# Output projection of a hybrid Conformer/MLA encoder: weights as two k tiles by 512 columns, products 512 wide, blocks, loads, norms and turns in another order

## The chip, the cores and the metric

The kernel runs on one core of one Trainium2 chip. Time is device time in microseconds (us), from the first to the last instruction of the program and what the launch adds around them. Three runs of the kernel before gave 1146.32, 1147.17 and 1148.84 us; the median is 1147.17 us. The engines are called PE (TensorE), DVE (VectorE), ACT (ScalarE), POOL (GpSimd) and SP (SyncE, which issues the loads and stores).

## The reference

Two sequences of 512 tokens with 16 meta tokens in front go through one encoder layer of width 1024. What matters here is the middle of it:

```python
u = jax.nn.silu(_layernorm(u, conv_ln_g[i], conv_ln_b[i]))        # 512 channels of the convolution
o = _mla_attention(...).reshape(b, l, MLA_HEADS * V_DIM)           # 512 channels of the attention
h = h + jnp.concatenate([u, o], axis=-1) @ w_out[i]                # output projection: 1024 x 1024
hf = _rms(h, ffn_norm_g[i])
h = h + (jax.nn.silu(hf @ w_gate[i]) * (hf @ w_up[i])) @ w_down[i] # feed-forward
```

Everything is float32. The meta tokens' rows are not needed behind the attention, so the output projection has 1024 tokens.

## The kernel before, in words

**Products.** A float32 product is made of three products of float32r parts: each operand is split in a high part (ACT, a cast) and a low part (DVE or POOL, a subtraction), and `mm3` (L151) issues high x high, high x low, low x high for every k tile of 128. All TensorE work of this kind stands under L158 in the profile. Names of a matmul are out<-moving,stationary.

**Output projection.** The stationary operand is 128 tokens by 128 channels of the mixed channels (`act`, or `cq` memory for the first sequence's attention channels), the moving operand is the weight. The weights are eight tiles of 128 x 1024, `wo[2 * dq + half]`: four k tiles by 256 output columns, `dq` being the quarter of the output columns and `half` the half of the channels (0 the convolution's, 1 the attention's). One `w_out_block(half, dq, t)` (L838) makes 128 tokens by 256 columns: 4 k tiles x 3 = 12 matmuls of 256 columns into one of four PSUM banks (`bank`), and DVE adds the result to the residual rows `hres[t]` (L844). There are 8 token tiles; tile t and tile t + 4 are the same rows of the two sequences. Tile 0 of the attention half is made ahead, between the steps of the last attention head (`early_blocks`, L718), in another PSUM tile, and added at L862.

**Weight buffers.** `pair` (L134) loads a tile (SP), casts it (ACT, L141) and subtracts (POOL, L144). Its high and low tiles have four buffers each (tags `pairh`, `pairl`), and a raw tile has two. The four weight tiles of the attention half are loaded during the attention; each of the other four takes a buffer whose user is done, behind each quarter of the attention half (L865). The feed-forward's operands (`Unit.comb`, L948) and the operands of the last stage use the same four and four buffers.

**Order.** First come the 28 blocks of the attention half (quarter by quarter, 7 token tiles), with the steps of the convolution's layer norm, its transposes and silu put between them by a table of positions 0 to 31 (L847-L865). Then come the 32 blocks of the convolution half (L1005-L1031), and between them:

- `ffn_norm(t)` (L876): store of the residual rows (SP), squares (ACT, L182), scale (POOL, L183 and L184), the normed rows in `hf2[t // 4]` (DVE, L881). There is one such tile for each sequence, so the norm of tile t + 1 waits for the turn of tile t.
- `ffn_turn(t)` (L883): 16 transposes on PE (L892) of the normed rows of t and t + 4, and the operands of the feed-forward's block products for these 128 tokens: copies and casts on ACT (L899, L903, L904, L913), sums and low parts on DVE (L900, L905, L908, L909, L911), low parts of four more on POOL (L914).
- `units[0].load()` and `units[0].comb(j)`: the seven weight operands of the feed-forward's first unit. For this unit the low halves are made on DVE (L961), for all later ones on POOL; four temporaries are made on DVE (L946).
- Behind the last norm the first unit's seven products over the tokens of turns 0 and 1 (256 columns), `ffn_turn(3)`, and then the same seven over the tokens of turns 2 and 3. From the second unit on, products are 512 columns wide.

The order written in the program is a priority: a planner that simulates a timeline orders the instructions of each engine, so an instruction whose operands are early can stand ahead of one written before it. [...]

## Time and profile before

| | before |
|---|---|
| median of three runs | 1147.17 us |
| span of the profiled execution | 1145.0 us |
| median less span (what lies around it) | 2.2 us |
| PE busy in the span | 1084.7 us, 95% |
| DVE busy | 828.9 us, 72% |
| POOL busy | 623.9 us, 54% |
| ACT busy | 522.2 us, 46% |
| output projection in the trace | first block at 363.4 us, last product at 463.2 us |
| first product 512 wide of the feed-forward | 497.1 us |

Times inside the profile are from the span's first instruction. A row of a timeline gives start, duration, engine, line, operation, names, shapes, and in brackets the idle time of the engine before it and what ended it. A row of a group gives count, busy time, mean duration in ns and the idle time before. [...]

### The profile page before, as it was taken

Reading aid. Unit: us, or ns where it says so; the run is one execution under the profiler, and the core shown is the slowest. Engines: PE = TensorE matmul, PEld = TensorE weight load, DVE = VectorE, ACT = ScalarE, POOL = GpSimd, SP = SyncE. Lnnn points to the kernel's source line nnn. Section 1 sums busy time; section 2 is a strip of 40 time slices with the busy share of each in tenths; the row PEclk is TensorE's granted clock in tenths of the full one; section 3 lists DMA queues with packets and bytes.
Section 4 is the critical chain, followed back from the end, with each engine's and each line's share of the span. In section 5 each row is a group of like instructions: output and inputs, shape, how many; then the busy total and the mean of one; then the engine's idle time right before and its main releaser. Section 6 shows DMA issues by size and latency. Waiting matters only on the chain. (4 is left out here: it accounts for less than half of the span.)

```text
span 1145.0 us, 15928 instructions
## 1 busy us (share of the span) xinstructions
PE 1084.7 (95%) x5886; PEld 931.5 (81%) x5886; DVE 828.9 (72%) x1142; ACT 522.2 (46%) x928; POOL 623.9 (54%) x499
## 2 busy tenths in 40 slices
PE   4999999999989999899999999999999999998797
PEld 4999887888878999788888888888888777787585
DVE  5699997888886547994555455545553868979998
ACT  6455525786874535643333333333333354343325
POOL 6489725563651323584544454445443586465955
PEclk9999999999999999899999999999999999999998
DMA  7211111010111312323231223122313963110103
GB/s 277 80 38 37 46 47 57 30 56 1 38 38 57 129 37 94 134 81 98 74 110 56 92 74 111 56 93 73 111 47 105 382 246 122 37 37 19 56 1 147
DMA packets 38556, 98.02 MB, mean 86 GB/s; under 512 B 4544, under 2 KB 4800, under 8 KB 38480
## 3 DMA queue, kind: packets, MB, share of 16 engines
q1 hardware_dynamic: 38480, 97.02, 25.0%
q8 instruction: 46, 0.75, 0.3%
q14 instruction: 30, 0.25, 0.1%
HBM read 77.08 MB, written 19.92 MB: 85 GB/s over the span
## 5 line engine op out<-in xcount | busy, mean ns | idle before, releaser
L158 PE MATMUL pt<-act_h,wc 128*128 128x512 f32 (+1 forms) x552 | 176.2, 382 | 0.1
L961 POOL TENSOR_TENSOR wc<-tt,wc 128x512 fp32r<-128x512 f32 x84 | 110.7, 1319 | 101.0 <-ACT wc L959 65.4
L1092 POOL TENSOR_TENSOR wd<-re,wd 128x512 fp32r<-128x512 f32 x69 | 113.4, 1660 | 51.4 <-ACT wd L1090 51.3
L959 ACT CAST wc<-tt 128x512 fp32r<-128x512 f32 x88 | 54.5, 622 | 152.9 <-PE pt L158 150.1
L158 PEld LDWEIGHTS pt<-act_h,wc 128*128 128x128 f32 x552 | 103.3, 190 | 19.9 <-issue 0.3
L158 PE MATMUL pt<-wd,wd 128*128 128x512 f32 x444 | 106.7, 395 | 9.0 <-DVE wd L1092 4.9
L158 PE MATMUL pt<-act_l,wc 128*128 128x512 f32 (+1 forms) x276 | 105.6, 383 | 3.5 <-DVE act_l L900 3.4
L158 PEld LDWEIGHTS pt<-wd,wd 128*128 128x128 f32 x444 | 84.1, 190 | 29.3 <-DVE wd L1092 6.2
L158 PE MATMUL ps<-wd,wd 128*128 128x512 f32 x396 | 96.1, 397 | 10.9 <-DVE wd L1092 7.3
L1090 ACT CAST wd<-re 128x512 fp32r<-128x512 f32 x120 | 68.2, 619 | 81.9 <-PE ps L158 29.9
L158 PEld LDWEIGHTS ps<-wd,wd 128*128 128x128 f32 x396 | 74.8, 191 | 29.7 <-DVE wd L1092 9.3
L144 POOL TENSOR_TENSOR wl<-raw,wh 128x1024 fp32r<-128x1024 f32 x28 | 68.8, 2456 | 51.3 <-ACT wh L141 51.1
L158 PE MATMUL pt<-hn_h,wh 128*128 128x256 f32 (+2 forms) x288 | 92.7, 324 | 1.1 <-ACT hn_h L148 1.1
L158 PE MATMUL pt<-hn_l,wh 128*128 128x256 f32 (+2 forms) x288 | 93.3, 324 | 0.0
L158 PE MATMUL pt<-hn_h,wl 128*128 128x256 f32 (+2 forms) x288 | 92.6, 322 | 0.0
L597 POOL TENSOR_SCALAR p<-p,sst 128x512 f32<-128x512 f32 x64 | 44.0, 693 | 67.2 <-DVE sst L595 59.3
L1092 DVE TENSOR_TENSOR wd<-re,wd 128x512 fp32r<-128x512 f32 x51 | 58.4, 1158 | 21.8 <-ACT wd L1090 21.8
L961 POOL TENSOR_TENSOR wc<-raw,wc 128x512 fp32r<-128x512 f32 x30 | 39.7, 1326 | 43.9 <-ACT wc L959 43.9
L158 PEld LDWEIGHTS pt<-act_l,wc 128*128 128x128 f32 x276 | 52.4, 190 | 13.6 <-DVE act_l L900 3.6
L314 POOL TENSOR_TENSOR pacc<-pacc,prod 128x512 f32<-128x512 f32 x43 | 58.3, 1355 | 7.0 <-ACT prod L312 4.3
L158 PEld LDWEIGHTS pt<-hn_h,wh 128*128 128x128 f32 x288 | 54.6, 191 | 6.0 <-ACT hn_h L148 1.5
L158 PE MATMUL pt<-s4h,wc 128*128 128x512 f32 (+1 forms) x184 | 58.4, 380 | 0.9 <-DVE h L976 0.9
(310 smaller groups left out, 3070.9 us busy)
## 6 DMA issues: line engine op xcount, KB each, us to landing
raw<-in_w_gate_dram SPq DMA_DIRECT2D x22, 512.0 KB, 3.7
g_dram<-slots SPq DMA_DIRECT2D x44, 256.0 KB, 2.4
re<-g_dram SPq DMA_DIRECT2D x40, 256.0 KB, 5.3
re<-in_w_down_dram SPq DMA_DIRECT2D x40, 256.0 KB, 5.4
raw<-in_w_in_dram SPq DMA_DIRECT2D x12, 512.0 KB, 3.9
slots<-in_w_up_dram SPq DMA_DIRECT2D x11, 512.0 KB, 3.5
h<-in_w_up_dram SPq DMA_DIRECT2D x11, 512.0 KB, 3.5
x<-in_x_dram SPq DMA_DIRECT2D x8, 512.0 KB, 5.0
```

The source lines that it names most:

```text
L144: nc.gpsimd.tensor_sub(lo[:, a], raw[:, a], hi[:, a].bitcast(F32))
L158: nc.tensor.matmul(out_ap, lhsT=w_, rhs=m_, start=first and i + j == 0, stop=last and i == n - 1 and j == 2)
L314: nc.gpsimd.tensor_add(acc, acc, to)
L597: nc.gpsimd.tensor_scalar(pr[:, real], pr[:, real], st[:, 2, t:t + 1], 1.0, op0=ALU.mult, op1=ALU.mult)
L959: nc.scalar.copy(w[:, 0:512], src)
L961: lo_eng.tensor_sub(w[:, 512:1024], src, w[:, 0:512].bitcast(F32))
L1090: nc.scalar.copy(w[:, 0:512], a)
L1092: eng.tensor_sub(w[:, 512:], a, w[:, 0:512].bitcast(F32))
```

## The change

The weight tiles become two k tiles by 512 columns, `wo[4 * half + 2 * e + k // 2]`, with `e` the half of the output columns; `w_out_rows` picks the k tile. A block is 128 tokens by 512 columns: again 12 matmuls and one add, each twice as wide, and half as many blocks. The tiles 4 to 7 (attention half) are loaded during the attention, two at a time, as before. Tiles 0 and 1 are loaded when the first column half of the attention blocks is done, tiles 2 and 3 when the second is. The layer norm's table keeps its positions; a block now stands for two. In the second part the blocks, `ffn_norm`, `ffn_turn` and `comb` are written in another order. The computation and its sums over k are the same.

```diff
+    def w_out_rows(half, e, k):
+        return tuple(wx[:, k % 2 * 512:(k % 2 + 1) * 512] for wx in wo[4 * half + 2 * e + k // 2])
...
-            for dq in range(4):
-                if dq == 0:
+            for e in range(2):
+                if e == 0:
                     early.append(bank2())
-                out_ap = early[t][:, dq // 2, dq % 2 * 256:(dq % 2 + 1) * 256]
                 cs = slice(t * 128, (t + 1) * 128)
-                for k0 in (0, 2):
-                    mm3(out_ap, [(o_first[0][:, k, cs], o_first[1][:, k, cs]) for k in (k0, k0 + 1)],
-                        [tuple(wx[:, k * 256:(k + 1) * 256] for wx in wo[2 * dq + 1]) for k in (k0, k0 + 1)],
-                        first=k0 == 0, last=k0 == 2)
+                for k in range(4):
+                    mm3(early[t][:, e, :], [(o_first[0][:, k, cs], o_first[1][:, k, cs])], [w_out_rows(1, e, k)],
+                        first=k == 0, last=k == 3)
                     yield
...
-            for n in (4 * WO_AT.index(h) + 1, 4 * WO_AT.index(h) + 3):
+            for n in (4 + 2 * WO_AT.index(h), 5 + 2 * WO_AT.index(h)):
                 wo[n] = pair(w_out[n])
...
-    def w_out_block(half, dq, t):
-        s, cs, ds = t // 4, slice(t % 4 * 128, t % 4 * 128 + 128), slice(dq * 256, (dq + 1) * 256)
+    def w_out_block(half, e, t):
+        s, cs, ds = t // 4, slice(t % 4 * 128, t % 4 * 128 + 128), slice(e * 512, (e + 1) * 512)
         pt = bank()
-        w = wo[2 * dq + half]
-        mm3(pt[:, :256], [(act[half][s][0][:, k, cs], act[half][s][1][:, k, cs]) for k in range(4)],
-            [tuple(wx[:, k * 256:(k + 1) * 256] for wx in w) for k in range(4)])
-        nc.vector.tensor_add(hres[t][:, ds], pt[:, :256], hres[t][:, ds])
+        mm3(pt, [(act[half][s][0][:, k, cs], act[half][s][1][:, k, cs]) for k in range(4)],
+            [w_out_rows(half, e, k) for k in range(4)])
+        nc.vector.tensor_add(hres[t][:, ds], pt, hres[t][:, ds])
...
-    for dq in range(4):
+    for e in range(2):
         for t in range(8):
             if t >= EARLY:
-                w_out_block(1, dq, t)
-            if dq * 8 + t >= EARLY_AT and early:
+                w_out_block(1, e, t)
+            at = 2 * (e * 8 + t)
+            if at >= EARLY_AT and early:
                 i = EARLY - len(early)
                 nc.vector.tensor_add(hres[i], early.pop(0).rearrange("p a b -> p (a b)"), hres[i])
-            for f, a in steps.pop(dq * 8 + t, ()):
+            for f, a in steps.pop(at, []) + steps.pop(at + 1, []):
                 f(*a)
-        wo[2 * dq] = pair(w_out[2 * dq])
+        for n in (2 * e, 2 * e + 1):
+            wo[n] = pair(w_out[n])
...
-    def w_out_rest(dqs, ts):
-        for dq in dqs:
-            for t in ts:
-                w_out_block(0, dq, t)
-
-    w_out_rest(range(3), (0, 4, 1, 5))
+    for t in (0, 4, 1, 5):
+        w_out_block(0, 0, t)
     for t in (0, 4):
-        w_out_block(0, 3, t)
+        w_out_block(0, 1, t)
         ffn_norm(t)
-    w_out_block(0, 3, 1)
-    w_out_block(0, 3, 5)
+    w_out_block(0, 1, 1)
+    w_out_block(0, 1, 5)
     ffn_turn(0)
     ffn_norm(1)
     ffn_norm(5)
     units[0].load()
-    w_out_rest((0,), (2, 6, 3, 7))
+    for t in (2, 6):
+        w_out_block(0, 0, t)
     ffn_turn(1)
     units[0].comb(0)
     units[0].comb(1)
-    w_out_rest((1,), (2, 6, 3, 7))
+    for t in (2, 6):
+        w_out_block(0, 1, t)
+        ffn_norm(t)
     units[0].comb(2)
     units[0].comb(3)
-    w_out_rest((2,), (2, 6, 3, 7))
-    w_out_block(0, 3, 2)
-    ffn_norm(2)
-    w_out_block(0, 3, 6)
-    ffn_norm(6)
-    w_out_block(0, 3, 3)
+    for t in (3, 7):
+        w_out_block(0, 0, t)
     ffn_turn(2)
-    ffn_norm(3)
-    w_out_block(0, 3, 7)
-    ffn_norm(7)
+    for t in (3, 7):
+        w_out_block(0, 1, t)
+        ffn_norm(t)
     for j in range(4, 7):
         units[0].comb(j)
     for j in range(7):
         units[0].product(j, slice(0, 256))
     ffn_turn(3)
     units[1].load()
...
-    w_out = _pack(a["w_out"][0], KD, 256).reshape(4, 128, 2, 1024).transpose(0, 2, 1, 3).reshape(8, 128, 1024)
+    w_out = np.ascontiguousarray(a["w_out"][0].reshape(2, 2, 2, 128, 2, 512).transpose(0, 4, 1, 3, 2, 5)).reshape(8, 128, 1024)
```

The rest of the diff takes comments and docstrings away.

## The prediction

> **What bounds the kernel now.** I read the page's engine totals first, then a table of stages around the output projection, then who PE waited for there, then the timelines of PE and DVE.

> ```profile
> span 1145.0 us, 15928 instructions
> PE 1084.7 (95%) x5886; PEld 931.5 (81%) x5886; DVE 828.9 (72%) x1142; ACT 522.2 (46%) x928; POOL 623.9 (54%) x499
> core 0: us, PE busy (x) PEld busy (x) DVE busy (x) ACT busy (x) POOL busy (x), PEclk, DMA share, GB/s
> 364.00:411.70 47.70, 46.95 (x394) 46.28 (x393) 26.64 (x61) 26.30 (x40) 12.73 (x17) 1.00 0.34 122
> 411.70:440.60 28.90, 28.90 (x245) 28.90 (x244) 14.06 (x28) 6.31 (x11) 5.15 (x7) 1.00 0.24 92
> 440.60:468.00 27.40, 25.82 (x216) 25.45 (x215) 27.34 (x38) 16.62 (x31) 14.59 (x14) 1.00 0.21 78
> 468.00:497.00 29.00, 22.05 (x162) 20.70 (x160) 27.96 (x34) 18.80 (x35) 17.88 (x16) 0.88 0.27 91
> 497.00:540.00 43.00, 42.93 (x189) 35.59 (x190) 28.45 (x34) 15.28 (x27) 27.22 (x20) 1.00 0.30 98
> ```

> The averages say PE. The stages say more: up to 440.6 us PE has no gap (28.90 of 28.90) and DVE is half idle. From 440.6 to 497.0 it is the other way round: DVE is busy 27.34 + 27.96 = 55.3 of 56.4 us, and PE stands still for 1.6 + 7.0 us, with a granted clock of 0.88. From 497 on PE is gapless again. So two limits follow each other: PE until the first turns, DVE until the second unit's products. Who ended PE's waits there:

> ```profile
> PE pt L158 <- DVE act_l L900: 3.4, 1, 3.4
> PE px L892 <- ACT act_h L899: 1.9, 1, 1.9
> PE pt L158 <- DVE h L844: 1.5, 1, 1.5
> PE pt L158 <- DVE h L976: 0.9, 1, 0.9
> ```

> All but one are DVE, and every one is a late instruction of a full list, not a slow one.

> **The products.** What one block costs is read from the spacing of blocks in a gapless stretch. DVE's adds follow PE block by block, and three blocks of 256 columns lie between these two rows; the PE rows below them are the first matmuls of two neighbouring products of 12 matmuls 512 columns wide.

> ```profile
> 426.27 0.42 DVE L844 TENSOR_TENSOR slots<-pt,slots 128x256 f32<-128x256 f32 x1 [1.02 <-PE pt L158]
> ...
> 430.59 0.42 DVE L844 TENSOR_TENSOR h<-pt,h 128x256 f32<-128x256 f32 x1 [1.02 <-PE pt L158]
> 551.58 0.39 PE L158 MATMUL pt<-s4h,wc 128*128 128x512 f32 x1
> ...
> 554.29 0.39 PE L158 MATMUL pt<-act_h,wc 128*128 128x512 f32 x1
> ```

> A narrow block is 4.32 / 3 = 1.44 us (120 ns a matmul), a wide one 2.71 us (226 ns). Two narrow ones against a wide one: 2.88 - 2.71 = 0.17 us. How many there are:

> ```profile
> L158 PE MATMUL pt<-wh,act_h 128*128 128x256 f32 x192 | 54.5, 285 | 1.6 <-DVE h L844 1.5
> L158 PE MATMUL pt<-wh,cq_h 128*128 128x256 f32 x48 | 13.8, 288 | 0.0
> L158 PE MATMUL ps<-wh,cq_h 128*128 128x256 f32 x16 | 4.6, 288 | 0.0
> ```

> Each row is one of the three parts, so 3 x 256 = 768 matmuls, 64 narrow blocks, become 32 wide ones: 32 x 0.17 = 5.4 us of PE's time, 2.7 us of it ahead of the second part (4 blocks made early and 28 of the attention half), 2.7 us in the second part. The bounds: nothing, if a wide matmul with these operands costs two narrow ones; 5.4 us by the rows. I take the rows, since the shapes are the same and only tile names differ. [...]

> **The adds.** Sixty adds of 256 columns become thirty of 512. Nearest rows for the wide add are the feed-forward's, PSUM plus SBUF, same shape:

> ```profile
> L844 DVE TENSOR_TENSOR slots<-pt,slots x40: 399/423/426, 374.7 to 466.6; 128x256 f32<-128x256 f32 x40
> L844 DVE TENSOR_TENSOR h<-pt,h x20: 409/417/425, 371.0 to 461.2; 128x256 f32<-128x256 f32 x20
> L994 DVE TENSOR_TENSOR slots<-pt,slots x33: 674/680/692, 512.7 to 902.3; 128x512 f32<-128x512 f32 x33
> ```

> 60 x 0.42 = 25.2 us against 30 x 0.68 = 20.4 us. In the crowded stretch, behind turn 0, stand 14 narrow adds (5.9 us) before and 8 wide ones (5.4 us) after: 0.5 us. DVE's list in its full stretch hardly gets shorter.

> **The loads.** Eight of 512 KB as before. The last one before the change was cast and subtracted when the attention half was done:

> ```profile
> 411.97 0.42 DVE L844 TENSOR_TENSOR slots<-pt,slots 128x256 f32<-128x256 f32 x1
> 412.12 1.05 ACT L141 CAST wh<-raw 128x1024 fp32r<-128x1024 f32 x1
> 413.25 2.60 POOL L144 TENSOR_TENSOR wl<-raw,wh 128x1024 fp32r<-128x1024 f32 x1 [7.99 <-ACT wh L141]
> ```

> Now two (tiles 2 and 3) come at that place: 1.05 + 2 x 2.5 = 6.1 us until the second low part. The first block that reads them is the fifth, 4 x 2.71 = 10.8 us on; the four blocks of column half 0 hide it with 4.7 us to spare, and if that cover were gone PE would wait 6.1 us. On SP the first unit's gate loads wait for these two raw tiles, the second of them one more subtraction (2.5 us); nothing on PE reads them before the first `comb`. The norms' stores move with the norms; on SP they stand behind those gate loads, which are out by 409.1 + 6.1 = 415.2 us, while the first norm comes some 14 us (five wide blocks) after 409.1. The two casts at the middle of the attention half put 5 us in a row on POOL ahead of the last layer norms' scales; PE has other blocks to do there, and I allow 0 to 1 us. I take these edits at nothing.

> **The order.** When does DVE's full stretch begin? With the first turn, whose two norms must be there:

> ```profile
> 432.03 0.42 DVE L844 TENSOR_TENSOR slots<-pt,slots 128x256 f32<-128x256 f32 x1 [1.01 <-PE pt L158]
> 435.29 1.29 DVE L881 SCALAR_TENSOR_TENSOR hf<-slots,rs,gain 128x1024 f32<-128x1024 f32 x1 [0.43 <-POOL rs L184]
> 436.99 1.04 PE L892 MATMUL px<-ident,hf 128*128 128x128 f32 x8
> ```

> Before: the residual of tile 4 is complete in its 14th block of the second part; from that add to the end of its norm it is 435.29 + 1.29 - 432.03 = 4.6 us, and the turn starts at 436.99. After: the attention half ends at 411.8 - 2.7 = 409.1 us. Tile 4 is complete with the sixth wide block, 409.1 + 6 x 2.71 = 425.4, its norm 0.3 + 4.6 us later, 430.3. The turn stands behind the eighth block on PE, 409.1 + 21.7 = 430.8, and its operands are just there. So the turn starts at 430.8 instead of 436.99: 6.2 us sooner, of which 3.5 us are the products and the rest the earlier norms.

> Behind it DVE has the same list (turns, norms, the first unit's combinations), 0.5 us shorter. If it stays full, its end moves with its beginning, and so does the second unit's first product:

> ```profile
> 497.07 0.47 PE L158 MATMUL pt<-act_h,wc 128*128 128x512 f32 x1
> ```

> It goes from 497.1 to about 490.9. Behind it the table has PE without a gap, so the shift goes through to the end.

> The sum: -6.2 for the stretch's start, -0.5 for the adds, +0.5 for the loads' bound and the new order's own small waits: -6.2 us. Against the span of 1145.0 us that is 1138.8; around the span lie 1147.17 - 1145.0 = 2.2 us, so **1141.0 us** as a median.

> **Rivals.**

> *PE becomes the bound: the stalls go as well.* PE's own work from the attention half's end is 16 x 2.71 + 8 groups of transposes at 0.8 (436.99 to the next matmul) + 14 products at 1.44 = 70.0 us; 409.1 + 70.0 = 479.1 instead of 497.1, 18 us less. For it: turn 2 now stands two wide blocks ahead of the end instead of one narrow one, so the last turns' chains start earlier. Against it: DVE's 55 us of work must then fit between 431 and 479. A third to two thirds of what lies between (8 to 14 us) gives 1133 to 1139. [...]

> *The first unit's operands come too late, and only the wide products' gain ahead of the turns remains.* Its seven weight operands need the four and four buffers that the projection's weights hold. Before, two came free with each quarter; now tiles 0 and 1 are read until block (0, 0, 7), the 14th of 16, and tiles 2 and 3 until the last. So four combinations written behind turn 1 can only be made some 8 us before the first product, and three only behind the last block.

> ```profile
> 447.16 0.68 DVE L961 TENSOR_TENSOR wc<-raw,wc 128x512 fp32r<-128x512 f32 x1
> ...
> 454.36 2.38 DVE L961 TENSOR_TENSOR wc<-tt,wc 128x512 fp32r<-128x512 f32 x2
> ...
> 462.99 0.28 PE L158 MATMUL pt<-act_h,wc 128*128 128x256 f32 x1
> ```

> Here the first ones were made at 447.16, 16 us before the first product at 462.99. DVE's work is not more by it, but PE would idle at the first products, in place of the waits of 1.9 and 3.4 us behind them. If PE then loses another 3 to 6 us, the gain is 0 to 3 us: 1144 to 1147.

> *Slower: DVE and POOL get in each other's way more often.* DVE's instructions with both operands in SBUF take much longer while POOL works:

> ```profile
> 440.66 0.69 DVE L900 TENSOR_TENSOR act_l<-h,act_h 128x512 fp32r<-128x512 f32 x1 [1.58 <-ACT act_h L899]
> 449.63 1.62 DVE L900 TENSOR_TENSOR act_l<-h,act_h 128x512 fp32r<-128x512 f32 x1
> 449.42 1.29 POOL L914 TENSOR_TENSOR s2l<-h,s2h 128x512 fp32r<-128x512 f32 x1 [3.26 <-ACT s2h L913]
> ```

> The same instruction takes 0.69 us with POOL idle and 1.62 beside L914: 0.9 us more. The change pushes seven L961 and the first unit's operands into the time in which turns 1 and 2 have POOL make low parts. The forecast's 6.2 us are gone with 7 more such meetings, and it is slower by more than noise from 10; 12 of them, of some 40 such instructions, give 1147.2 - 6.2 + 10.8 = 1152.

> *Wide products cost two narrow ones.* The lower bound above: the attention half then ends at 411.8 as before, the eighth block at 411.8 + 23.0 = 434.8, and the turn is 2.2 us sooner by the order alone, 1145.0. Against it stands every product behind 497 us, at 226 ns. [...]

> *The change doesn't do what it says.* The planner may order blocks, norms and turns otherwise than written, and only the products' 5.4 us, or part of them, would show. It lies inside the forecast's range.

> **How the numbers follow.** Forecast (a gain of 3 to 8 us, 1139 to 1144): 0.57. PE bound (more than 8): 0.15. Late operands (0 to 3): 0.16. Wide products at twice the price (1145): 0.03. Slower: 0.09. The range reaches from 1136.0 (half of the PE case) to 1147.0 (all of the late operands). A difference of 0.2%, 2.3 us, is about what a measurement of this kernel can tell. Below 1144.9 lie the forecast, the PE case and a quarter of the late operands: 0.76. Within 0.2%: the rest of the late operands, the twice-price case and a little of the slower case: 0.16. Slower: 0.08.

> **What the profile after would show.** Products: 384 matmuls of 128x512 in the projection, spaced 226 ns; at twice 120 ns the 5.4 us are wrong. Adds: 30 of 128x512 at 0.68. Loads: PE never waits for L141 or L144. Order: the first L892 near 431 us, the full stretch of DVE from about 434 to 491, the first wide feed-forward product near 491. If that product moves far more than the first L892, PE was the bound; if it moves less, the waits say whether it was L961 (late operands) or long L900, L908 and L961 beside POOL. Wrong altogether: a gap of PE in the attention half, or a stage behind 540 us that changes its own length by more than 1 us.

## The result, and the profile after

The changed kernel takes 1155.68 us as a median (1153.76 to 1155.80); the kernel before, timed beside it, 1148.01 us (1146.32 to 1149.06). The ratio is 1.0068, with a 95% interval of 1.0055 to 1.0081: **slower by 7.8 us**, where 1141.0 us and a gain of 6.2 us had been forecast. The profiled execution of the changed kernel took 1153.76 us and spans 1152.0 us; that of the kernel before spans 1145.0 us, so the profiles show 7.0 us of it.

The lines of the program have moved by one to three: the residual's add is L845, the norm's transposes L805 and back L825, its copy back L826, the silu L830 with its parts L832 and L833, the turn's transposes L895, the unit's temporaries L949, its low parts L964, the sums behind the products L979 to L993.

The table of stages of the changed kernel, cut at the attention half's last instruction on PE, the first turn, the first unit's middle and the second unit's first product (columns: stretch, length, busy time of PE, PEld, DVE, ACT and POOL with the count of instructions, granted clock, that is the share of TensorE's full clock, DMA share, GB/s):

```profile
span 1152.0 us, 15137 instructions
364.00:408.40 44.40, 44.40 (x222) 36.77 (x221) 21.19 (x41) 19.43 (x28) 13.33 (x14) 1.00 0.33 115
408.40:439.80 31.40, 24.44 (x100) 19.50 (x98) 13.94 (x22) 9.91 (x16) 3.83 (x9) 0.84 0.21 82
439.80:468.00 28.20, 27.09 (x146) 23.01 (x145) 23.97 (x25) 19.81 (x35) 14.82 (x15) 1.00 0.14 57
468.00:501.70 33.70, 25.60 (x182) 24.39 (x181) 32.55 (x44) 18.74 (x36) 22.01 (x15) 0.89 0.36 118
501.70:545.00 43.30, 43.30 (x186) 35.67 (x186) 26.99 (x31) 14.06 (x25) 25.01 (x19) 0.96 0.28 91
```

The second row is new. Before, PE had no gap from 411.7 us to the first turn and beyond; now it stands still for 7.0 us there, at a clock of 0.84. Whom PE waited for between 400 and 505 us (total, times, longest; the two smallest left out):

```profile
PE pt L158 <- ACT act_h L832: 4.1, 1, 4.1
PE pt L158 <- DVE h L979: 3.3, 1, 3.3
PE ps L825 <- ACT xs L817: 2.8, 2, 2.5
PE pt L158 <- DVE slots L993: 2.2, 1, 2.2
PE pt L158 <- DVE wc L964: 1.1, 1, 1.1
PE pt L158 <- POOL s1l L917: 1.1, 1, 1.1
```

The first and the third row are the convolution's layer norm, which cost PE nothing worth naming before (0.7 us for one of its transposes). The second row stood in the table before with 0.9 us, as `h` of L976. The runs below that take these three waits away, and with them the halved clock behind, win back the loss and more.

Where the 7.0 us of the profiles arise, by three marks:

| | before | after | difference | forecast |
|---|---|---|---|---|
| first turn's first transpose | 436.99 | 439.77 | +2.8 | -6.2 |
| from there to the second unit's first product | 60.1 | 61.7 | +1.6 | 0 (-0.5 + 0.5) |
| from there to the end of the span | 647.9 | 650.5 | +2.6 | 0 |

So the forecast missed by 9.0 us ahead of the first turn, by 1.6 in the crowded stretch, and by 2.6 behind it. The first mark is kind to the changed kernel: the profile before has a stretch at half clock at 340.2 us, ahead of the projection, which the one after lacks. A later profile of the kernel before with one edit behind the first turn (the last run below) has no such stretch, the same list up to there, and its first turn at 435.53 us.

### The profile page after: what moved, and what is told of

It is laid out like the page before. It is cut to its first block, busy times and chain, and to the rows that moved or that the text cites. A ratio compares the mean times of both kernels' runs of the same rounds, so it can differ in the third digit from the quotient of the medians.

```text
span 1152.0 us, 15137 instructions
## 1 busy us (share of the span) xinstructions
PE 1086.5 (94%) x5502; PEld 916.3 (80%) x5502; DVE 823.1 (71%) x1112; ACT 522.2 (45%) x928; POOL 628.6 (55%) x499
## 5 line engine op out<-in xcount | busy, mean ns | idle before, releaser
L158 PE MATMUL pt<-act_h,wc 128*128 128x512 f32 (+1 forms) x552 | 177.8, 385 | 1.7 <-DVE wc L964 1.1
L964 POOL TENSOR_TENSOR wc<-tt,wc 128x512 fp32r<-128x512 f32 x84 | 110.6, 1317 | 103.0 <-ACT wc L962 69.7
L158 PEld LDWEIGHTS pt<-act_h,wc 128*128 128x128 f32 x552 | 104.4, 192 | 22.4 <-DVE wc L964 1.3
L158 PE MATMUL pt<-wd,wd 128*128 128x512 f32 x444 | 108.0, 399 | 8.7 <-DVE wd L1090 4.8
L158 PEld LDWEIGHTS pt<-wd,wd 128*128 128x128 f32 x444 | 85.3, 193 | 29.2 <-DVE wd L1090 6.1
L158 PE MATMUL pt<-act_l,wc 128*128 128x512 f32 (+1 forms) x276 | 106.4, 385 | 0.9 <-DVE act_l L903 0.9
L158 PE MATMUL ps<-wd,wd 128*128 128x512 f32 x396 | 96.9, 400 | 10.1 <-DVE wd L1090 7.3
L158 PEld LDWEIGHTS ps<-wd,wd 128*128 128x128 f32 x396 | 76.1, 193 | 28.6 <-DVE wd L1090 9.3
L158 PE MATMUL pt<-hn_h,wh 128*128 128x256 f32 (+2 forms) x288 | 92.8, 324 | 1.1 <-ACT hn_h L148 1.1
L158 PE MATMUL pt<-hn_l,wh 128*128 128x256 f32 (+2 forms) x288 | 93.5, 325 | 0.0
L158 PE MATMUL pt<-hn_h,wl 128*128 128x256 f32 (+2 forms) x288 | 92.9, 323 | 0.0
L144 POOL TENSOR_TENSOR wl<-raw,wh 128x1024 fp32r<-128x1024 f32 x28 | 68.5, 2447 | 41.4 <-ACT wh L141 41.1
L1090 DVE TENSOR_TENSOR wd<-re,wd 128x512 fp32r<-128x512 f32 x51 | 60.9, 1204 | 19.8 <-ACT wd L1088 19.7
L964 POOL TENSOR_TENSOR wc<-raw,wc 128x512 fp32r<-128x512 f32 x30 | 39.1, 1306 | 44.3 <-ACT wc L962 44.3
L158 PEld LDWEIGHTS pt<-act_l,wc 128*128 128x128 f32 x276 | 53.0, 192 | 11.0 <-DVE act_l L903 1.1
L158 PE MATMUL pt<-s4h,wc 128*128 128x512 f32 (+1 forms) x184 | 58.5, 381 | 3.3 <-DVE h L979 3.3
L158 PE MATMUL pt<-a12h,wc 128*128 128x512 f32 (+1 forms) x184 | 59.4, 385 | 2.2 <-DVE slots L993 2.2
```

The costliest lines, as they stand in the source:

```text
L144: nc.gpsimd.tensor_sub(lo[:, a], raw[:, a], hi[:, a].bitcast(F32))
L158: nc.tensor.matmul(out_ap, lhsT=w_, rhs=m_, start=first and i + j == 0, stop=last and i == n - 1 and j == 2)
L964: lo_eng.tensor_sub(w[:, 512:1024], src, w[:, 0:512].bitcast(F32))
L1090: eng.tensor_sub(w[:, 512:], a, w[:, 0:512].bitcast(F32))
```

## The experiments

Medians are compared by their ratio to the kernel before, timed in the same series; a difference of two ratios is turned into us with 1147 us, and is uncertain by about 2 us, since each interval is some 1.4 us to either side. The kernel before gave 1145.16, 1146.87 and 1147.33 us in the three later series, against 1148.01 beside the changed kernel, which was not timed again; plain differences of medians are therefore up to 2.9 us larger than the differences given here. A second measure is the profile's two marks: the first turn (439.77 in the changed kernel) and the second unit's first product (501.49); the first one moved by 1.5 us between two profiles with the same list up to there (above).

Three theories came first. **A**: the layer norm's chain (transposes, statistics, scale, normed rows, transposes back, silu) stands later in PE's list than before, and PE runs out of other blocks before it ends. **B**: the new order of blocks, turns and combinations in the second part costs the time. **C**: POOL's two subtractions for the weight tiles hold the norm's scales. D, E and F came out of the first results.

### The transposes back in the product banks

The layer norm's transposes and the transposes back share two wide PSUM tiles (`bank2`). `LB_T` moves the transposes back to the four banks of the products.

```diff
-LB_T = False
+LB_T = True
```

> The changed kernel with one constant set: the layer norm's back transposes write to the four product banks (tag t) instead of the two wide PSUM tiles (tag s) that they share with the norm's own transposes. Theory A (the layer norm chain, short of PSUM tiles and placed late by the planner, makes PE wait 7 us at 409 to 417 us and at half clock for 3 us more; the rest of the change is worth what was forecast): the wait goes, the first FFN turn starts at 431 to 433 us instead of 439.8, the time is 9 to 13 us under the changed kernel, 2 to 6 us under the kernel before. Theory B (the new order of norms, turns and combinations costs the time in the last stretch): the first turn starts sooner, but the second unit starts no sooner than 499 us, the time stays over the kernel before by 4 us or more. Theory C (two POOL subtractions of the last weight tiles in a row hold up the norm): as A, since the chain is then over before those subtractions.

Measured: 1150.34 us, ratio 1.0047 (1.0034 to 1.0059): 2.4 us less than the changed kernel. The first turn starts at 436.63, 3.1 us sooner, the second unit's first product at 498.87. The norm's transposes are now early, the last of them back at 399.9 us instead of 412.1, and the 4.1 us for `act_h` are gone. But PE waited 3.5 and 0.8 us for the normed rows of two token tiles, the first of which ACT made only behind the first sequence's silu and casts (383.7 to 389.8 us), and the clock halved for one stretch of 3.4 us (a mean of 0.85 from 385.0 to 396.7 us). Theory A names the right chain, but its gain (9 to 13 us) was put far too high: taking the banks away only moved the wait to the chain's next link, ACT. That is theory **D**.

The same edit on the kernel before:

```diff
-LB_T = False
+LB_T = True
```

> The kernel before with the same one constant as e1 and nothing else. Theories A and C: there the chain was over before the attention half ended (PE had no gap in 375 to 440 us), so nothing is won: within 1.5 us of the kernel before. If it gains as much as e1 gains over the changed kernel, e1 says nothing about the change.

Measured: 1154.10 us, ratio 1.0085 (1.0072 to 1.0099), 9.7 us *slower* than without the edit. I had expected nothing. PE waited 1.3 us for normed rows and 1.0 us more than before for the residual's adds, which free the banks that products and transposes back now share; the first turn moved from 436.99 to 439.77. And a wait for `h` of L976 went from 0.9 to 3.2 us, the same as in the changed kernel, though the second part has the old order here. This was the first sign that the 3.3 us wait does not need the new order.

### Narrow products in the attention half, then everywhere

The changed kernel, with each block of the attention half issued as two times 256 columns into the same bank:

```diff
-        mm3(pt, [(act[half][s][0][:, k, cs], act[half][s][1][:, k, cs]) for k in range(4)],
-            [w_out_rows(half, e, k) for k in range(4)])
+        for a in ((slice(0, 256), slice(256, 512)) if half == 1 else (slice(0, 512),)):
+            mm3(pt[:, a], [(act[half][s][0][:, k, cs], act[half][s][1][:, k, cs]) for k in range(4)],
+                [tuple(w[:, a] for w in w_out_rows(half, e, k)) for k in range(4)])
```

> The changed kernel, but each block of the attention half issued as two sums of 256 columns into the two halves of its bank; weights, loads, positions of the norm's steps and the whole second part stay. Theory A: the planner takes two narrow products for much longer than one wide one, so the same positions give an earlier norm in PE's list; the wait of 7 us shrinks to under 2 us, the narrow products cost 14 x 0.17 = 2.4 us, the sum is 5 to 9 us under the changed kernel. Theory B: 2.4 us over the changed kernel. Theory C: the wait stays at 3 us or more, as the POOL subtractions stand where they stood; 0 to 3 us under the changed kernel.

Measured: 1149.87 us, ratio 1.0042 (1.0028 to 1.0056): 3.0 us *less* than with wide products. PE's 14 blocks of this half take 14 x 0.17 = 2.4 us more by the forecast's spacing, and yet it is at the first turn 4.3 us sooner, at 435.44. The planner ordered anew: the norm's last transposes are at 404.4 us instead of 408.4, and PE's wait at the half's end is 2.1 us instead of 7.0, with no halved clock behind it (wide matmuls there start 0.23 us apart, at 415.69 and 415.92 us). Theory A's 5 to 9 us are missed all the same, and 3.0 us lies at the edge of C's 0 to 3, though C's wait of 3 us or more did not stay. The width of the products alone, with the program's order untouched, moves the norm in PE's list, and the norm costs more than the width saves.

And all blocks as two times 256 columns, on top of the transposes back in the product banks:

```diff
-LB_T = False
+LB_T = True
...
-        mm3(pt, [(act[half][s][0][:, k, cs], act[half][s][1][:, k, cs]) for k in range(4)],
-            [w_out_rows(half, e, k) for k in range(4)])
+        for a in ((slice(0, 256), slice(256, 512)) if True else (slice(0, 512),)):
+            mm3(pt[:, a], [(act[half][s][0][:, k, cs], act[half][s][1][:, k, cs]) for k in range(4)],
+                [tuple(w[:, a] for w in w_out_rows(half, e, k)) for k in range(4)])
```

> e1 with all blocks of the projection outside the early one issued as two sums of 256 columns, layout, loads and order as in the change. What the width alone is worth once the norm is out of the way: 30 x 0.17 = 5.1 us of PE time, of which 2.4 us lie ahead of the second part. Theory A: 2.5 to 5 us over e1 (all of it if PE bounds, the part up to the first turn, 3.7 us, if DVE does). If width is worth nothing on the chip: equal to e1 within 1.5 us.

Measured: 1153.18 us, ratio 1.0073 (1.0059 to 1.0087), 3.0 us more than the same kernel with wide products; the first turn is 1.5 us later, at 438.09. So wide products are worth something here, but less than the 5.1 us that the spacing gives for these 30 blocks. The planner ordered anew in this run too, and PE's waits for the normed rows are 6.3 us instead of 4.3, so the 3.0 us are not the width alone.

### The norm's first transposes in the product banks

`LN_T` moves the other half of the norm's PSUM use: the first transposes go to the product banks, the transposes back keep the two wide tiles for themselves.

```diff
-LN_T = False
+LN_T = True
```

> The changed kernel, but the layer norm's first transposes (not those back) go through the four product banks instead of the two wide PSUM tiles. Theory A (the chain of the layer norm is late because its two transposes share two wide PSUM tiles, and PE waits for its end): the last transposes back then stand 13 wide blocks into PE's list instead of 17 (the attention half ends at 16), so the 2.5 and 4.1 us waits at the end of the attention half go, and the three half-clock windows behind them; the first turn near 431 to 433 us, the time 1144 to 1148, 8 to 12 us under the changed kernel. Theory D (ACT is what holds the chain: with the banks of the transposes back changed, PE still waited 3.5 and 0.8 us for them behind ACT's silu and casts of the first sequence): a wait of 2 to 4 us stays near 390 us, first turn 435 to 437, time 1149 to 1151. Theory B (the new order of the second part costs the time): the first turn may move, but the time stays within 2 us of the changed kernel, 1153 to 1156.

Measured: 1147.32 us, ratio 0.9998 (0.9987 to 1.0009): 8.0 us less than the changed kernel, level with the kernel before. The first turn starts at 432.71. The table of stages and PE's waits from 400 us on, of this run:

```profile
364.00:405.50 41.50, 39.46 (x204) 32.36 (x203) 25.49 (x45) 23.37 (x35) 12.12 (x18) 1.00 0.34 123
405.50:432.70 27.20, 27.20 (x121) 22.48 (x120) 14.01 (x20) 6.79 (x11) 6.33 (x6) 1.00 0.27 97
432.70:461.00 28.30, 27.21 (x147) 23.11 (x146) 24.03 (x26) 19.80 (x35) 14.80 (x15) 1.00 0.14 56
461.00:494.90 33.90, 25.71 (x182) 24.28 (x179) 32.47 (x44) 18.87 (x36) 22.95 (x16) 0.91 0.36 124
```

```profile
PE pt L158 <- DVE h L979: 3.3, 1, 3.3
PE pt L158 <- DVE slots L993: 2.2, 1, 2.2
```

The smaller rows, from 1.1 us down, are left out. Both rows of the norm are gone, and PE has no gap from 405.5 us to the first turn, at full clock. Theory A's forecast for the turn (431 to 433) and the time hold; D's waits of 2 to 4 us did not come (0.3 and 0.3 us), because the list spreads them: the last three transposes back are at 391.7, 398.1 and 401.6 us, each about a wide block or more behind the one before; B falls, since its order is untouched here. But the stretch from the first turn on is 62.2 us, no shorter than in the changed kernel: a second cause is left.

### The old order of the second part

Behind the first turn, blocks, turns, norms and combinations as in the kernel before, as far as two column halves allow it where there were four quarters; on top of the run above:

```diff
-    for t in (2, 6):
+    for t in (2, 6, 3, 7):
         w_out_block(0, 0, t)
     ffn_turn(1)
-    units[0].comb(0)
-    units[0].comb(1)
-    for t in (2, 6):
-        w_out_block(0, 1, t)
-        ffn_norm(t)
-    units[0].comb(2)
-    units[0].comb(3)
-    for t in (3, 7):
-        w_out_block(0, 0, t)
+    for j in range(4):
+        units[0].comb(j)
+    w_out_block(0, 1, 2)
+    ffn_norm(2)
+    w_out_block(0, 1, 6)
+    ffn_norm(6)
+    w_out_block(0, 1, 3)
     ffn_turn(2)
-    for t in (3, 7):
-        w_out_block(0, 1, t)
-        ffn_norm(t)
+    ffn_norm(3)
+    w_out_block(0, 1, 7)
+    ffn_norm(7)
```

> As the run with the norm's first transposes in the product banks, with the second part of the projection in the old order behind the first turn (four blocks, turn, four combinations, then the last blocks with their norms, the third turn ahead of the last block but one). Theory B: the stretch from the first turn to the second unit's first product falls from 61.9 us to 60 or less, the wait of 3.3 us for the last sum's operand goes to about 1 us as in the kernel before, and the time is 2 to 5 us under the run beside it. Theory A: the order matters by at most 1.5 us either way.

Measured: 1150.33 us, ratio 1.0028 (1.0015 to 1.0040), 3.4 us *more* than the run above. The stretch from the first turn to the second unit's first product is 66.1 us instead of 62.2, with waits of 3.1 us for a norm of the third turn and 2.5 us for a high part of the fourth. Theory B has the sign wrong: the new order is the better one here, and by more than the 1.5 us that theory A allowed.

### The low parts of the weights on DVE

Theory C takes its strength from these rows of the changed kernel, where POOL's two subtractions stand ahead of a norm's scale that DVE had ready at 406.09 us:

```profile
404.34 4.74 POOL L144 TENSOR_TENSOR wl<-raw,wh 128x1024 fp32r<-128x1024 f32 x2 [2.95 <-ACT wh L141]
409.16 0.23 POOL L813 TENSOR_SCALAR brs<-bag 128x1 f32<-128x1 f32 x1
```

The edit makes the low parts of tiles 0 to 3 on DVE, through a new argument of `pair`:

```diff
-            wo[n] = pair(w_out[n])
+            wo[n] = pair(w_out[n], eng=nc.vector)
```

> The changed kernel, with the low parts of weight tiles 0 to 3 made on DVE instead of POOL, so that POOL does nothing but the norm's scales there. Theory C (two subtractions of 4.74 us on POOL hold the last norms' scales by 2.4 and 3.1 us): the wait before the first block of the second sequence falls from 4.1 to 1.5 us or less, and the time falls by 3 to 6 us, to 1150 to 1153. Theory A: the place of the norms in PE's list is as before, at 16 and 17 blocks, so PE still waits 4 us or more in all at the end of the attention half, and DVE has four subtractions more, two of them just ahead of the crowded stretch: within 2 us of the changed kernel, 1153.5 to 1157.5.

Measured: 1154.11 us, ratio 1.0062 (1.0047 to 1.0077), within 1 us of the changed kernel. The wait for `act_h` is 4.14 us as before, and 2.8 us for the normed rows. The scale's delay of 3.1 us is real, but the last token tile's norm does not wait for it: its first transposes stand at 408.03 us in PE's list (409.27 in this run), and everything behind them follows from there. C falls.

The same on top of the norm's first transposes in the product banks (the edits of both runs):

```diff
-LN_T = False
+LN_T = True
...
-            wo[n] = pair(w_out[n])
+            wo[n] = pair(w_out[n], eng=nc.vector)
```

> Both: the norm's first transposes in the product banks and the low parts of weight tiles 0 to 3 on DVE. Theory C: 2 to 4 us under the run with the banks alone, since the two last norms' scales stand behind POOL's subtractions there too. Theory A: within 1.5 us of the run with the banks alone.

Measured: 1147.20 us, ratio 1.0001 (0.9989 to 1.0012), the same as without it, as theory A expected.

### The second unit's temporaries

What is left is the 3.3 us wait for L979. It stands in every run so far with the new order (2.2 us in the one with narrow products throughout) and in the kernel before with the transposes back moved, but with only 0.9 us in the kernel before itself, and not in the run with the old order. DVE's timeline in the run with the norm's first transposes moved (start, duration, line, names):

```profile
484.27 0.68 DVE L917 TENSOR_TENSOR s2l<-slots,s2h 128x512 fp32r<-128x512 f32 x1
484.87 1.78 DVE L949 TENSOR_TENSOR tt<-slots,h 128x512 f32<-128x512 f32 x1
486.69 1.67 DVE L949 TENSOR_TENSOR tt<-slots,tt 128x512 f32<-128x512 f32 x1
488.28 1.77 DVE L949 TENSOR_TENSOR tt<-slots 128x512 f32<-128x512 f32 x1
489.97 1.75 DVE L949 TENSOR_TENSOR tt<-h,tt 128x512 f32<-128x512 f32 x1
491.64 0.41 DVE L979 TENSOR_TENSOR h<-pt,h 128x256 f32<-128x256 f32 x1
492.20 0.55 PE L158 MATMUL pt<-s4h,wc 128*128 128x256 f32 x1 [3.29 <-DVE h L979]
```

And the same place in the kernel before:

```profile
493.12 1.78 DVE L946 TENSOR_TENSOR tt<-slots 128x512 f32<-128x512 f32 x1
494.82 0.41 DVE L976 TENSOR_TENSOR h<-pt,h 128x256 f32<-128x256 f32 x1
495.16 1.43 DVE L946 TENSOR_TENSOR tt<-h,tt 128x512 f32<-128x512 f32 x1
```

DVE is done with the last turn's operands and starts the temporaries at 484.87 us, 5.2 us sooner than before (490.05). It then makes the *second* unit's four temporaries, 6.8 us in a row, and only then the sum of a product of the first unit that PE had already finished. PE's last product needs the bank which that sum frees. In the kernel before, the sum stood ahead of the fourth temporary. In the kernel before with the transposes back moved, all four stand ahead of it (492.51 to 499.36 us), and PE waits 3.2 us. That this order of DVE's list costs the time is theory **E**. Its rival **F**: POOL, which makes the second unit's low parts, sets the end of the stretch anyhow.

The edit makes the first two of these four temporaries on POOL, on top of the run with the norm's first transposes moved:

```diff
-            nc.vector.tensor_sub(self.t[n], x_, y_)
+            (nc.gpsimd if self.u == 1 and n in ("t1", "t2") else nc.vector).tensor_sub(self.t[n], x_, y_)
```

> The run with the norm's first transposes in the product banks, and the first two of the second unit's four temporaries (L949) made on POOL instead of DVE; the computation is the same. There DVE made all four in a row (484.9 to 491.6 us) ahead of the sum of the first unit's fourth product (L979), and PE waited 3.29 us for the bank that this sum frees. Theory E (this order of DVE's list costs the second half of the missing gain): the sum then stands behind one temporary, the wait of 3.3 us falls to under 1 us, the second unit's first product goes from 494.9 to 490.5 to 492, the time falls by 2 to 4 us, to 1143.5 to 1145.5. Rival F (POOL's low parts of the second unit set that end): two more subtractions on POOL put the third weight operand at 497 us or later, PE waits 1 to 4 us there instead, and the time stays within 1.5 us.

Measured: 1143.23 us, ratio 0.9967 (0.9953 to 0.9980): **3.8 us less than the kernel before**, 11.6 less than the changed one. Of this run, the timeline around the wait and the table of stages:

```profile
485.86 1.79 DVE L949 TENSOR_TENSOR tt<-slots 128x512 f32<-128x512 f32 x1
488.62 0.42 DVE L979 TENSOR_TENSOR h<-pt,h 128x256 f32<-128x256 f32 x1 [0.98 <-PE pt L158]
...
489.74 0.28 PE L158 MATMUL pt<-s4h,wc 128*128 128x256 f32 x1
...
491.53 0.40 PE L158 MATMUL pt<-act_h,wc 128*128 128x512 f32 x1
493.77 4.71 POOL L964 TENSOR_TENSOR wc<-tt,wc 128x512 fp32r<-128x512 f32 x3
```

```profile
433.70:462.00 28.30, 27.20 (x147) 23.08 (x146) 24.03 (x27) 19.81 (x35) 14.82 (x15) 1.00 0.14 56
462.00:491.50 29.50, 24.45 (x181) 23.04 (x180) 27.57 (x41) 16.51 (x32) 18.58 (x14) 0.94 0.36 125
491.50:540.00 48.50, 48.50 (x216) 40.07 (x215) 33.78 (x36) 17.59 (x30) 36.74 (x25) 1.00 0.31 104
```

Now DVE waits for PE (0.98 us) where PE waited 3.29 for DVE. The stretch is 57.8 us instead of 62.2, and PE has no gap behind 491.5: POOL's low parts are not late although POOL has two subtractions more. E holds, F falls.

With the first and the third temporary on POOL instead:

```diff
-            (nc.gpsimd if self.u == 1 and n in ("t1", "t2") else nc.vector).tensor_sub(self.t[n], x_, y_)
+            (nc.gpsimd if self.u == 1 and n in ("t1", "t3") else nc.vector).tensor_sub(self.t[n], x_, y_)
```

> As the run beside it, with the first and the third temporary on POOL. DVE's sum then stands behind one temporary that itself waits for POOL's, at about 489 us instead of 491.6; POOL has the third operand some 1.5 us earlier than with the first and second. Theory E: the wait falls from 3.3 to about 1 us, the time to 1143.5 to 1145.5. Rival F: PE waits less at the third operand than in the run beside it, and this one is the faster by 1 us or more.

Measured: 1143.84 us, ratio 0.9973 (0.9962 to 0.9985), with a wait of 0.7 us for L979: the same as the run beside it within the intervals, so F's second claim falls as well.

The edit on the changed kernel itself, the norm untouched:

```diff
-            nc.vector.tensor_sub(self.t[n], x_, y_)
+            (nc.gpsimd if self.u == 1 and n in ("t1", "t2") else nc.vector).tensor_sub(self.t[n], x_, y_)
```

> The changed kernel itself, with the first two of the second unit's four temporaries on POOL. Theory E: the wait of 3.29 us before the last sums' product goes here too, without the norm being touched: 2 to 4 us under the changed kernel, 1151.5 to 1153.5. Rival F: within 1.5 us of it, 1154 to 1157.

Measured: 1147.94 us, ratio 1.0011 (1.0000 to 1.0022): 6.5 us less than the changed kernel, more than E's 2 to 4. The stretch from the first turn is 57.8 us instead of 61.7, and the one from there to the next wait of PE (near 910 us) is 2.0 us shorter: the changed kernel runs its first 3.4 us of products there at half clock (501.40 to 504.81 us), and this run does not. Another 1.0 us of the profile lies ahead of the first turn (438.77 us), where the edit changes nothing and one stretch of 3.4 us less ran at half clock; that part is luck. The mean clock of the profiled execution is 0.986, against 0.983 in the changed kernel. The norm's waits (4.1 and 2.8 us) are as they were.

And on the kernel before:

```diff
-            nc.vector.tensor_sub(self.t[n], x_, y_)
+            (nc.gpsimd if self.u == 1 and n in ("t1", "t2") else nc.vector).tensor_sub(self.t[n], x_, y_)
```

> The kernel before, with the first two of the second unit's four temporaries on POOL. There the wait at this place was 0.93 us and DVE made only three of the four ahead of the sum, so theory E gives at most 1 us; two more subtractions on POOL may cost as much: within 1.5 us of the kernel before either way. If it gains 2 us or more, the temporaries held the kernel before as well, and they are no reason why the changed one is slower.

Measured: 1146.02 us, ratio 0.9991 (0.9980 to 1.0001), 1.0 us less than the kernel before, which the interval does not tell from nothing. Its wait of 0.9 us is gone, and there was little more to gain: all four temporaries ahead of the sum are a loss of the changed kernel, not of the kernel before. Why the planner puts them there is not shown; it does so as well in the kernel before with the transposes back moved, so neither the wide products nor the new order is needed for it.

The two repairs do not add: alone they are worth 8.0 and 6.5 us, together 11.6. With the temporaries on POOL in both kernels, the change with the norm's first transposes moved is 2.8 us under the kernel before (1143.23 against 1146.02 us, same series). One control is missing: the kernel before with the norm's first transposes moved was not run. Its PE has 0.75 us of idle time from 364.0 to 411.7 us and none from there to 440.6, so there is little to gain by its waits, but what the planner would make of the edit is open.

## Why the prediction was wrong, step by step

**The products: right.** The projection has 384 matmuls of 512 columns and thirty adds of 0.69 us. One row of each, from the groups by line of the changed kernel:

```profile
L158 PE MATMUL pt<-wh,act_h 128*128 128x512 f32 x96 | 39.3, 409 | 4.1 <-ACT act_h L832 4.1
L845 DVE TENSOR_TENSOR slots<-pt,slots 128x512 f32<-128x512 f32 x19 | 13.1, 688 | 16.0 <-PE pt L158 14.3 <-DMA slots<-in_x_dram 1.7
```

PE's rows in its timeline start 0.227 us apart (435.23 to 435.46 to 435.68) and are 0.39 us long each: the durations overlap, so the spacing is what a block costs. The attention half's list ends at 408.6 us, where 409.1 was forecast. It holds 180 matmuls of 512 columns, 15 blocks and not 14, so one block of the convolution half is in it; only two groups of transposes back (0.36 us each in a gapless list) stand behind. With these two put in order, PE's work ahead of the second part ends at 406.6 us, 5.2 us sooner than before. Of these, 1.9 us lie ahead of the first block (361.53 instead of 363.42 us, mostly the half clock of the profile before), 0.7 us are a wait that is gone, and some 2.5 are the 14 blocks, for which 14 x 0.17 = 2.4 was forecast. One sum of the prediction is off without changing its result: of the turn's 6.2 us the products are 2.7 + 8 x 0.17 = 4.1, not 3.5, which agrees with the 2.2 that it gives to the order alone.

**The step that failed** is the sentence of the loads about the layer norm: "PE has other blocks to do there, and I allow 0 to 1 us". It was argued for POOL's subtractions alone, and for those it is right (the two runs with the low parts on DVE). But the norm as a whole was never followed: nowhere did I ask where its transposes stand among blocks that are half as many and twice as long. In the kernel before, the eighth tile's norm was transposed back at 406.0 us, 5.8 us ahead of the half's end (the first row below, from the profile before). In the changed one this is the chain:

```profile
405.95 0.60 PE L823 MATMUL ps<-ident,xs 128*128 128x128 f32 x4
...
408.03 0.49 PE L805 MATMUL ps<-ident,U 128*128 128x128 f32 x3
...
411.09 0.66 PE L825 MATMUL ps<-ident,xs 128*128 128x128 f32 x4 [2.46 <-ACT xs L817]
412.11 0.66 PE L825 MATMUL ps<-ident,xs 128*128 128x128 f32 x4 [0.36 <-ACT xs L817]
...
413.42 2.93 ACT L830 ACTIVATE U<-U,sm 128x512 f32<-128x512 f32 x4
416.25 2.16 ACT L832 CAST act_h<-U 128x512 fp32r<-128x512 f32 x4
416.90 0.79 PE L158 MATMUL pt<-wh,act_h 128*128 128x512 f32 x1 [4.14 <-ACT act_h L832]
```

The last norm's first transposes are the last thing PE does before it runs dry. From there to the second sequence's first operand lie 8.3 us of DVE, POOL, ACT, PE and ACT again, and PE has nothing else to do: 2.46 + 0.36 + 4.14 = 7.0 us, where 0 to 1 was allowed. The products behind that wait run at a granted clock of 0.50 until 422.9 us, which costs another 3.0 us (half of the 6.0 us that PE is busy there, an estimate). Those 10 us are the 9.0 us by which the first turn missed its forecast and 1.0 by which PE was otherwise early: its work up to there 2.5 us sooner than forecast, mostly by the clock of the profile before, against 0.9 us for the turn standing a third of a block later (22 blocks and 4 matmuls behind the first) and 0.6 for two groups of transposes that do not overlap products (0.66 us each instead of 0.36). With the norm's first transposes in other banks the turn starts at 432.7 us, 1.9 us from the forecast's 430.8. What the planner's reasons are for putting the norm there is not shown; that the width of the products alone moves it by 4 us is (the run with narrow products in the attention half).

**The order: half right.** "Behind it DVE has the same list ... If it stays full, its end moves with its beginning" held for DVE: it was done with the last turn's operands 5.2 us sooner in the run with the norm moved. It failed for PE, because the list is not in the same order. The planner put all four temporaries of the second unit ahead of the first unit's last sums, where three had stood, so that of the 5.2 us some 2.2 were left at the second unit's first product (494.90 instead of 497.07). With both repaired this product starts at 491.53, where 490.9 was forecast, and the time is 1143.2 us, where 1141.0 was.

**The rivals.** *PE becomes the bound*: no; PE's idle time in the crowded stretch grew from 8.6 to 9.2 us. *Late operands*: the wait for L964 is there, but it is 1.1 us in place of 3 to 6. *Slower: DVE and POOL get in each other's way*: its sign came out, its mechanism did not. Between the two marks (to 0.2 us) DVE is busy 23.97 + 32.55 = 56.5 us in the changed kernel. The kernel before, its stages cut at the same marks:

```profile
436.99:468.00 31.01, 29.43 (x248) 29.06 (x247) 28.02 (x40) 19.16 (x34) 14.90 (x15) 1.00 0.23 86
468.00:497.07 29.07, 22.05 (x162) 20.73 (x161) 28.00 (x35) 18.87 (x35) 17.95 (x16) 0.88 0.27 91
```

That is 28.02 + 28.00 = 56.0 us, so DVE's work grew by 0.5 us where the rival needs 6 and more. *Twice the price*: no, by the spacing above (0.227 us where twice the narrow one is 0.240). *The change doesn't do what it says*: this was the one to work out. I wrote that the planner "may order blocks, norms and turns otherwise than written" and then let it cost only part of the gain. It did order the norm and the temporaries otherwise, and repairing either won about what the change had to give, 8.0 and 6.5 us against 6.2.

**Wrong altogether** was to be "a gap of PE in the attention half, or a stage behind 540 us that changes its own length by more than 1 us". Both came true, the first just: PE stands still right behind the half's last products. The second is the clock. Of the 2.6 us behind the second unit's first product, 1.5 come with a stretch at half speed at 501.4 us and 1.6 with one at 1091.9 us, which lengthens the last stage (from PE's 3.3 us wait near the end) from 59.2 to 60.8 us; the stages between give 0.5 back. The profile before has neither stretch.

## What the runs showed of the clock

```profile
405.84:409.25 3.41, 2.79 (x17) 2.11 (x15) 1.24 (x4) 0.59 (x1) 3.33 (x3) 1.00 0.40 118
409.25:412.67 3.42, 1.22 (x8) 0.84 (x8) 0.78 (x4) 2.03 (x3) 1.49 (x4) 1.00 0.54 189
412.67:416.08 3.41, 0.09 (x1) 0.00 (x0) 0.00 (x0) 3.25 (x5) 0.00 (x0) 0.50 0.00 0
416.08:419.49 3.41, 2.59 (x6) 2.10 (x7) 2.52 (x5) 2.33 (x5) 0.00 (x0) 0.50 0.00 0
419.49:422.91 3.42, 3.42 (x9) 2.65 (x9) 2.57 (x4) 0.00 (x0) 0.00 (x0) 0.50 0.00 0
422.91:426.32 3.41, 3.41 (x16) 2.82 (x16) 0.69 (x1) 0.00 (x0) 0.00 (x0) 1.00 0.00 0
...
1088.50:1091.90 3.40, 0.70 (x3) 0.62 (x4) 3.40 (x4) 0.00 (x0) 3.40 (x3) 1.00 0.00 0
1091.90:1095.30 3.40, 3.40 (x10) 2.62 (x9) 3.40 (x2) 0.80 (x2) 3.40 (x3) 0.50 0.00 0
```

The kernel before has the same wait near the end, 3.28 us, but there it lies across the border of two periods:

```profile
1080.86:1084.27 3.41, 1.66 (x8) 1.03 (x6) 3.41 (x4) 1.14 (x2) 3.41 (x3) 1.00 0.00 0
1084.27:1087.68 3.41, 1.89 (x8) 1.59 (x9) 3.41 (x3) 0.00 (x0) 3.41 (x3) 1.00 0.00 0
```

What the two profiles show, cut into such periods from their first record of the clock on (22.73 and 23.53 us): 13 periods at full clock are followed by one at half clock, and PE is busy in 5 to 45% of them (1.22 of 3.42 us above); 628 are followed by another at full clock, and PE is busy in 48% of them or more (1.66 of 3.41 us in the kernel before, above). What makes the clock change is not shown, and the limits are those of these two executions. A wait of 2.2 us was followed by half clock here (the one for L993 in the changed kernel, which ends at 484.12 us: from 480.92 to 484.33 us PE is busy for 1.14 of 3.41 us, and the next two periods run at half), and one of 3.28 us was not. Of the half periods, those that PE is busy for 3, 14, 74 and 76% of the time (from 412.67 us in the changed kernel, 480.12 in the kernel before, 484.33 and 416.08 in the changed one) are followed by another half one; the eleven that are 92% busy or more are followed by full clock. By the spacings of 0.427 and 0.227 us a period full of products at half clock costs 1.6 us, and of the two waits near the end only the one of 3.25 us, whose period is 21% busy (0.70 of 3.40 us), was followed by half clock; the periods with the wait of 3.28 us are 49 and 55% busy. This fits the spread of one kernel: in the last series the kernel before took 1144.5 to 1147.0 us in the twelve executions with a mean clock of 0.991 or more, and 1147.7 to 1149.7 us in the eleven with 0.987 or less.

In the profile before, the half clock ahead of the second unit does not begin with the wait of 3.4 us for `act_l`. That wait ends at 483.06 us, and the half clock begins at 480.12: the period before it, 38% busy with the wait of 1.9 us in it, stands ahead of the first half period, and most of the wait of 3.4 us lies in that first one (busy for 0.47 of 3.41 us), ahead of the second. The changed kernel has 0.9 us in place of that wait, and still two half periods there (484.33 to 491.16 us).

## What to carry to other kernels

When the length of an instruction changes in a list that a planner orders, follow every chain that is threaded through that list, not only the work that was edited: its last link is what the next stage waits for. Ask of each engine's list which sum frees a bank or a buffer, and whether work for a later stage has slipped ahead of it. And price a wait on PE by the granted clock of its profile as well: here the 6.8 us behind a wait of 2.2 us ran at 0.50, where a full 3.41 us of products costs 1.6 us more.
